# A decoder layer on one core: the FFN's first weights, factors and products as routines of the attention's event loop

## The chip, the core and the metric

The kernel runs on one core of a Trainium2 chip. The metric is the time of one execution on the device in microseconds (us). The core has five engines with instruction streams of their own: TensorE (PE in the profile; its weight loads are PEld), VectorE (DVE), ScalarE (ACT), GpSimd (POOL) and SyncE (SP, which here only issues transfers; ScalarE issues some too). Each engine works through its stream in order and waits on semaphores for the others.

## The reference, cut to what matters

One layer on 2048 tokens of width 1024, all in float32:

```python
h = rms_norm(x, norm1_g)
proj = h @ w_in
o_a = swa_sink_mixer(qa, ka, va, sinks, bias)        # 256 columns, window of 128
o_b = s5_mixer(proj[...], ...)                       # 512 columns, state space model + GLU
o_c = nsa_mixer(qc, kvc, gc, ...)                    # 256 columns: compressed, selected, window of 512
mixed = concat([rms_norm(o_a, g_a), rms_norm(o_b, g_b), rms_norm(o_c, g_c)])
x = x + mixed @ w_out
h2 = rms_norm(x, norm2_g)
hid = relu(h2 @ w_up)                                # 4096 columns
out = x + (hid * hid) @ w_down
```

## The kernel before, in words

Every float32 product is made of three matmuls: each operand is split into a high part (a cast to the matmul format on ScalarE) and a low part (a subtraction on VectorE), and high x high, high x low and low x high are added in PSUM. `split` (L1910) is this pair of instructions.

**Stages.** `phase_front` makes the projection and the state space model. A bias stage in `trunk` (L2365 on) makes the position biases, the windowed attention of group A and part of the GLU; its loads stand on SP's queue. `phase_mix` (L1156) makes the attention of group C (16 blocks of 128 queries), the last six blocks of the GLU and the output projection (16 "rows" of 128 tokens). `phase_up` (L1916) and `phase_down` (L2157) make the FFN.

**The event loop.** `phase_mix` writes its order out by hand. `Flow` (L1067) is a small planner that runs while the program is built. Every piece of work is a generator that yields `(engine, ns, function)` for a step, an `Event` to wait for, or a `Ring` (a number of buffers) to take a place of. `run` always takes the ready step with the earliest start by its costs, and among equals the one with the lowest rank. The calls of the functions in that order are the program's order on each engine (`tc.manual_schedule`); the costs serve for nothing else, and on the chip each engine waits for the real data. What is traced after that block (`phase_up`) is placed by the compiler's own scheduler, which may move it ahead between the instructions of the loop, in the order of its priority.

**The opening.** When the GLU is done, `opening` (L1230) runs `open_late` (L1200) as one step of VectorE with 5000 ns: it releases the GLU's memory, opens the pools of the output projection on the left side of SBUF, loads two vectors of gains (`g2t`, `wo_g`), makes two inverse roots of 16 numbers a partition on VectorE (`rsqrt_into`, L55, for group A's and B's norms), and sends the second through HBM to turn its layout (`r_d`, `r_t`, then `turn_rows` L1224 on TensorE). Then the 16 pieces of `w_out` are loaded and split (`weighed`, L1246).

**A row.** `finished(i)` (L1711) waits for the attention's output of block i in HBM (`oc`) and for the one buffer `mix`, loads 256 + 512 + 256 columns, scales the first two parts on POOL, squares the third on ScalarE into a tile `sq`, makes its inverse root on POOL (2300 ns in the plan), scales it, and turns the row in two halves on TensorE (bank `pt`), each split into `mh` and `ml`. `filled(i)` (L1759) makes 48 matmuls into two half rows, one bank `pw` each (L1781); for rows 14 and 15 the second half takes a bank `pq` of the attention. `added` (L1796) adds x on VectorE (L1803) and squares the sum on ScalarE with its output into the same PSUM bank (L1804); only then is the bank given back. `posted` (L1808) stores the row, makes the inverse root of the second norm, and for rows 0 to 7 turns and stores the normed row for the FFN.

Rows have a high rank number (100 i + 400 for i < 14), so that their matmuls fill gaps of the attention; some are left when the attention ends.

**The FFN.** Seven products of a Strassen-like scheme for each pair of 512 x 512 blocks, in the order 1, 6, 7, 5, 2, 4, 3. `fetch_factor` (L1996) loads a factor of the tokens (`fx`, 1 MB) from `hT` or `sums`, `refill` (L2000) splits it (`fh`, `fl`, 128x2048 each). `weights` (L2019) loads four blocks of `w_up` (`ur`), forms four sums on POOL (`fs`, L2037) and splits seven operands (`uh`, `ul`). `up` (L2052) makes the products: twelve matmuls each (L2066), into banks a, d, c, b (`pua` and so on). The first two factor fetches have a raised priority (`UP_HOIST`), and the compiler's scheduler also moves the first splits and weights ahead into the last rows.

## Time and profile before

| | us |
|---|---|
| median of 3 runs | 2488.86 (2485.08 to 2491.16) |
| the profiled execution | 2486.98 |
| its span, first to last instruction | 2484.9 |
| PE busy | 2397.5 |
| DVE busy | 1779.7 |
| ACT busy | 1321.3 |
| POOL busy | 1036.7 |

Times in the trace count from the first instruction. The opening lies at about 646, the end of the attention at about 1184, the FFN's first matmul at 1237 and the first of `phase_down` near 1880. In the lists of instructions a line gives the start, the length, the engine, the line of the code, the operation and out<-in; in square brackets stands how long the engine had been idle and what it then got. ACTq and SPq are transfers issued by ScalarE and SP. Matmuls are pipelined, so their lengths overlap: a 128x512 matmul at full clock starts about 0.23 us after the one before and is listed with 0.39.

### The profile page before, as it was taken

The numbers are of one execution on the slowest core, as the hardware profiler recorded it, in microseconds if no ns is written. First come the engines' busy times: TensorE is split into PE (matmuls) and PEld (weight loads), VectorE is DVE, ScalarE is ACT, GpSimd is POOL, SyncE is SP. The second block draws the span as 40 slices with busy tenths as digits, with TensorE's granted clock in tenths as the row PEclk, the third lists the DMA queues.
The fourth block names the chain that finished last, engine by engine and source line by source line (L and its number), as shares of the span: only waits on it lengthen the run. The fifth ranks groups of instructions, "written<-read, shape, count | busy, mean of one in ns | idle before, by whom it ended". The sixth has DMA issues, their size and how long they took to land.

```text
span 2484.9 us, 37987 instructions
## 1 busy us (share of the span) xinstructions
PE 2397.5 (96%) x12738; PEld 2059.6 (83%) x12738; DVE 1779.7 (72%) x3493; ACT 1321.3 (53%) x2756; POOL 1036.7 (42%) x1041
## 2 busy tenths in 40 slices
PE   8999998999899999999799999999999999999999
PEld 7899997777788888888688888788887888888887
DVE  7853875864777888888465566655557888889886
ACT  6443555765667767666355555444444444434442
POOL 0000223322243444231666674666654444445447
PEclk9999999999899999999999999999999999999999
DMA  7473334341322243212566667655548443444435
GB/s 233 137 257 118 105 99 108 105 149 48 112 76 71 85 127 111 67 39 68 166 204 193 191 191 225 207 152 151 153 130 287 133 124 97 132 139 127 127 102 196
DMA packets 402259, 344.45 MB, mean 139 GB/s; under 512 B 43622, under 2 KB 359020, under 8 KB 400112
## 3 DMA queue, kind: packets, MB, share of 16 engines
q1 hardware_dynamic: 341696, 288.23, 38.4%
q10 hardware_dynamic: 60368, 53.80, 6.9%
q8 instruction: 100, 1.64, 0.3%
q14 instruction: 95, 0.78, 0.1%
HBM read 227.39 MB, written 119.76 MB: 140 GB/s over the span
## 4 chain that ended last, share of the span: by engine, by line
PE 68%; DVE 3%; issue 3%; POOL 2%; DMA 2%; ACT 1%; ACTq 0%; SPq 0%; DVEq 0%; POOLq 0%
PE pdc L2245 7%; PE pdb L2245 7%; PE pda L2245 7%; PE pub L2066 6%; PE puc L2066 6%; PE pw L1781 6%; PE pua L2066 6%; PE pdd L2245 3%; PE pud L2066 3%; PE pos L1481 2%; PE pps L1448 2%; PE pow L1481 1%; PE pqs L1424 1%; PE pqs L1423 1%; PE ppw L1448 1%
## 5 line engine op out<-in xcount | busy, mean ns | idle before, releaser
L1912 ACT CAST v<-vr 128x512 fp32r<-128x512 f32 x224 | 139.3, 623 | 304.0 <-DMA vr<-vd 156.7
L1913 DVE TENSOR_TENSOR v<-vr,v 128x512 fp32r<-128x512 f32 x224 | 240.4, 1082 | 78.3 <-ACT v L1912 78.1
L2245 PE MATMUL pdc<-dw,v 128*128 128x512 f32 x768 | 187.3, 393 | 4.2 <-ACT dw L1912 2.8
L2245 PE MATMUL pdb<-dw,v 128*128 128x512 f32 x768 | 184.5, 389 | 0.0
L2245 PE MATMUL pda<-dw,v 128*128 128x512 f32 x768 | 184.5, 389 | 0.0
L2245 PEld LDWEIGHTS pdc<-dw,v 128*128 128x128 f32 x768 | 145.5, 190 | 36.0 <-ACT dw L1912 3.2
L548 POOL TENSOR_TENSOR t<-Q,E 128x508 f32<-128x508 f32 x16 | 22.1, 1381 | 364.5 <-ACT Q L528 326.4
L2245 PEld LDWEIGHTS pdb<-dw,v 128*128 128x128 f32 x768 | 144.2, 188 | 30.0
L2245 PEld LDWEIGHTS pda<-dw,v 128*128 128x128 f32 x768 | 144.2, 188 | 29.9
L1912 ACT CAST uh<-fs 128x512 fp32r<-128x512 f32 x124 | 76.3, 621 | 156.9 <-PE pub L2066 58.7
L1913 DVE TENSOR_TENSOR ul<-fs,uh 128x512 fp32r<-128x512 f32 x124 | 128.8, 1040 | 33.4 <-ACT uh L1912 33.1
L2037 POOL TENSOR_TENSOR fs<-ur,ur 128x512 f32<-128x512 f32 x62 | 86.8, 1400 | 156.0 <-DMA ur<-in_w_up 138.5
L1913 DVE TENSOR_TENSOR ul<-ur,uh 128x512 fp32r<-128x512 f32 x93 | 97.6, 1051 | 43.7 <-ACT uh L1912 41.1
L1781 PE MATMUL pw<-wo_h,mh 128*128 128x512 f32 x256 | 105.5, 412 | 10.4 <-ACT pw L1804 10.2
L2082 POOL TENSOR_TENSOR ev<-e,e 128x512 f32<-128x512 f32 x64 | 95.4, 1490 | 47.9 <-ACT e L2079 20.4
L1464 ACT CAST ths<-pps 128x512 fp32r<-128x512 f32 (+1 forms) x144 | 79.2, 563 | 64.5 <-PE pps L1448 53.9
L1469 DVE TENSOR_TENSOR tls<-pps,ths 128x512 fp32r<-128x512 f32 (+1 forms) x144 | 92.8, 657 | 17.2 <-ACT ths L1464 16.0
L1781 PE MATMUL pw<-wo_h,ml 128*128 128x512 f32 x256 | 104.3, 408 | 0.0
L2066 PE MATMUL pub<-fh,uh 128*128 128x512 f32 x256 | 101.1, 395 | 3.0 <-DVE e L2075 3.0
L1781 PE MATMUL pw<-wo_l,mh 128*128 128x512 f32 x256 | 103.7, 405 | 0.0
L2066 PE MATMUL puc<-fh,uh 128*128 128x512 f32 x256 | 100.2, 391 | 1.9 <-DVE eu L2075 1.9
L2066 PE MATMUL pua<-fh,uh 128*128 128x512 f32 x256 | 99.8, 390 | 1.5 <-ACT pw L1804 1.5
(560 smaller groups left out, 7777.7 us busy)
## 6 DMA issues: line engine op xcount, KB each, us to landing
vr<-vd SPq DMA_DIRECT2D x224, 256.0 KB
vd<-ev SPq DMA_DIRECT2D x128, 256.0 KB
ur<-in_w_up SPq DMA_DIRECT2D x124, 256.0 KB
vd<-e ACTq DMA_DIRECT2D x64, 256.0 KB
dr<-in_w_down SPq DMA_DIRECT2D x32, 512.0 KB
x<-in_x SPq DMA_DIRECT2D x16, 512.0 KB
mx<-in_x ACTq DMA_DIRECT2D x32, 256.0 KB
x<-mx ACTq DMA_DIRECT2D x32, 256.0 KB
```

The costliest lines, as they stand in the source:

```text
L1423: nc.tensor.matmul(pq[:, o:o + w], S["qA"][:, h], ka, start=True, stop=False)
L1448: nc.tensor.transpose(pt[:, j, hh], sls[hh][:, (b0 + j) * P:(b0 + j + 1) * P], C["ident"])
L1464: yield "ACT", cast_ns(n), lambda: nc.scalar.copy(th[:, 0:nb], pt[:, 0:nb])
L1469: t = yield "DVE", sub_ns(n), lambda: nc.vector.tensor_tensor(tl[:, 0:nb], pt[:, 0:nb], th[:, 0:nb], op=ALU.subtract)
L1481: nc.tensor.matmul(po_of(), v_of(b0 + j), tt[:, j].rearrange("p h q -> p (h q)"), start=b0 + j == 0 and n == 0, stop=b0 + j == nblk - 1 an ...
L1781: t = yield "PE", mm_ns(512), lambda: nc.tensor.matmul(pw[n], a[half][:, j], b[k][:, sl], start=k == 0 and m == 0, stop=k == NK - 1 and m ...
L1912: nc.scalar.copy(dh, src)
L1913: nc.vector.tensor_tensor(dl, src, dh, op=ALU.subtract)
L2037: nc.gpsimd.tensor_tensor(t, x, y, op=op)
L2066: nc.tensor.matmul(bank[b], w[:, k], h[o][:, k], start=first and k == 0 and n == 0, stop=k == HALF - 1 and n == 2, skip_group_check=True)
L2082: nc.gpsimd.tensor_tensor(tile_("v" + o), x, y, op=op)
L2245: nc.tensor.matmul(bank[b, q], x[:, q, j], y[:, j], start=first and j == 0 and n == 0, stop=j == 1 and n == 2, skip_group_check=True)
```

## The change: what it does

- `open_late` becomes a step of ScalarE's queue with 60 ns and only opens pools, now on the right side of SBUF. The gains are loaded once, in the bias stage (`gs`). The two inverse roots run on POOL in a routine `norms`; the turned one first.
- `finished` loads the first 768 columns of a row as soon as `mix` is free; the third part has a routine of its own (`load_oc`) that waits for the attention's output.
- The squares of a row write their unused output to a tile `junk` in SBUF. The bank `pw` is given back after the addition. Rows 14 and 15 no longer use the attention's banks.
- `attention_over` waits for the last block's output, closes the attention's pools and the biases' (`over`), opens a second `pw` bank and a new `pt` bank, and runs `phase_up`, now a generator, up to its first `yield`. Its weights, the fetches of five factors, the splits of three factors (in quarters) and the products 1, 6 and 7 are then routines of the event loop with the rank 100000 and more; the weight sums wait until row 15's first half is turned. Product banks come from two pools of four.
- The rest of `phase_up` is traced after the loop as before. `UP_HOIST` is gone.

```diff
-def phase_mix(tc, C, x, gains, B, cmp, w_out, out_norm_g, g2, pd, ..., oc_d, glu, release):
+def phase_mix(tc, C, x, gains, B, cmp, w_out, out_norm_g, g2, pd, ..., oc_d, glu, release, over, up):
...
+        def late_pool(name, bufs, **kw):
+            return ctx.enter_context(tc.tile_pool(name=name, bufs=bufs, reuse_waits="tile", side="right", **kw))
...
         def open_late():
 
             release()
-            fp = late["fp"] = pool("m_f", 1)
-            wp = pool("m_w", 1)
-            late["ps"] = pool("m_psw", 1, space=PSUM)
-            ps_o.append(pool("m_pso2", 1, space=PSUM))
+            fp = late["fp"] = late_pool("m_f", 1)
+            wp = late_pool("m_w", 1)
+            late["sm"] = late_pool("m_sml", 3)
+            late["small"] = small_of(late["sm"])
+            ps_w.append(late_pool("m_psw", 1, space=PSUM))
+            ps_o.append(pool("m_pso2", 1, space=PSUM, side="right"))
...
-            g2t = late["g2"] = fp.tile([P, NK], F32, name="g2t")
-            nc.sync.dma_start(g2t, g2[0].rearrange("(k p) -> p k", p=P))
-            go = late["go"] = wp.tile([P, NK], F32, name="wo_g")
-            nc.sync.dma_start(go, out_norm_g[0].rearrange("(k p) -> p k", p=P))
-            ra, rc = (fp.tile([P, NT], F32, name=n) for n in ("r_a", "r_c"))
-            rsqrt_into(nc, sm, ra, ss_a, 1.0 / 256, NT, "ra")
-            rsqrt_into(nc, sm, rc, ss_b, 0.25 / 512, NT, "ra")
-            nc.vector.tensor_scalar(rc, rc, 0.5, None, op0=ALU.mult)
-            nc.sync.dma_start(r_d.rearrange("(c s) -> c s", s=T16), rc)
+            late["junk"] = fp.tile([P, 512], F32, name="junk")
+
+        def row_norms():
+            rsqrt_into(nc, late["sm"], late["rc"], ss_b, 0.25 / 512, NT, "ra", nc.gpsimd)
+            nc.gpsimd.tensor_scalar(late["rc"], late["rc"], 0.5, 1.0, op0=ALU.mult, op1=ALU.mult)
...
-            yield "DVE", 5000, open_late
-            put(R["po"], flow.engines["DVE"])
-            fire(opened, flow.engines["DVE"])
+            t = yield "ACT", 60, open_late
+            put(R["po"], t)
+            spawn(norms(), 55, t)
+            fire(opened, t)
...
+        def norms():
+            yield "POOL", 3300, row_norms
+            t = yield "SP", 60, row_norms_out
+            spawn(rows_turned(), 60, t + 2 * DMA_NS)
+            yield "POOL", 3100, lambda: rsqrt_into(nc, late["sm"], late["ra"], ss_a, 1.0 / 256, NT, "ra", nc.gpsimd)
+            fire(norms_there, flow.engines["POOL"])
...
             yield opened
             box = {}
-            yield ev["oc"]
             yield R["mix"]
...
-                nc.scalar.dma_start(mix[:, 768:D], oc_d[rows])
-            t = yield "ACT", 180, load
+            t = yield "ACT", 120, load
+            spawn(load_oc(i, rows, box), rank, t)
...
+            yield box["oc"]
             dst = mix[:, 768:D]
...
-            yield "ACT", 630, lambda: nc.scalar.activation(sq, dst, AF.Square, accum_out=ss)
+            yield "ACT", 630, lambda: nc.scalar.activation(late["junk"][:, 0:256], dst, AF.Square, accum_out=ss)
...
+        def load_oc(i, rows, box):
+            box["oc"] = Event()
+            yield E[i]["oc"]
+            t = yield "ACT", 60, lambda: nc.scalar.dma_start(box["mix"][:, 768:D], oc_d[rows])
+            fire(box["oc"], t + DMA_NS + 700)
...
-                    alt = i >= ENDING and n
-                    yield R["pq"] if alt else R["pw"]
-                    p, tag, bufs = (ps_s, "pq", 2) if alt else (late["ps"], "pw", 1)
-                    pw[n] = p.tile([P, 512], F32, tag=tag, bufs=bufs, name=f"pw{i}{n}")
+                    yield R["pw"]
+                    bank = ps_w.pop(0)
+                    pw[n] = bank.tile([P, 512], F32, tag="pw", name=f"pw{i}{n}")
...
-            yield "DVE", 683, lambda: nc.vector.tensor_tensor(xt, xt, pw, op=ALU.add)
-            t = yield "ACT", 789, lambda: nc.scalar.activation(pw, xt, AF.Square, accum_out=ss[:, n:n + 1])
-            put(R["pq" if alt else "pw"], t)
+            t = yield "DVE", 683, lambda: nc.vector.tensor_tensor(xt, xt, pw, op=ALU.add)
+            ps_w.append(bank)
+            put(R["pw"], t)
+            t = yield "ACT", 820, lambda: nc.scalar.activation(late["junk"], xt, AF.Square, accum_out=ss[:, n:n + 1])
             fire(done, t)
...
+        def attention_over():
+
+            yield E[NT - 1]["oc"]
+            yield R["pt"]
+            box = {}
+
+            def switch():
+                c_att.close()
+                over()
+                ps_t[0] = late_pool("m_pst2", 1, space=PSUM)
+                ps_w.append(late_pool("m_psw2", 1, space=PSUM))
+                box.update(next(up))
+            t = yield "SP", 30, switch
+            put(R["pt"], t)
+            put(R["pw"], t)
+            first = {o: Event() for o in ORDER[:3]}
+            kept = {o: Event() for o in ORDER[:3]}
+            spawn(ffn_weights(box, kept), R_FFN, t)
+            prev = None
+            for o in ORDER[:5]:
+                spawn(ffn_factor(box, o, prev, first.get(o)), R_FFN + ORDER.index(o), t)
+                prev = first.get(o)
+            for o in ORDER[:3]:
+                spawn(ffn_product(box, o, first[o], kept[o]), R_FFN + ORDER.index(o), t)
+
+        def ffn_factor(box, o, prev, done):
+            yield R["fx"]
+            t = yield "SP", 60, lambda: box["fetch"](o)
+            if done is None:
+                return
+            yield landing(t, 1e6)
+            if prev is not None:
+                yield prev
+            box["slot"](o)
+            for k in range(HALF):
+                yield "ACT", 621, lambda: box["high"](o, k)
+                t = yield "DVE", 1060, lambda: box["low"](o, k)
+            put(R["fx"], t)
+            fire(done, t)
+
+        def ffn_weights(box, kept):
+            t = yield "SP", 240, box["load"]
+            yield landing(t, 1e6)
+            for o, n in box["weights"]:
+                if n is not None:
+                    yield E[NT - 1]["mh", 0]
+                    yield "POOL", 1440, n
+                spawn(ffn_kept(box, o, kept.get(o)), R_FFN + ORDER.index(o), flow.engines["POOL"] if n else flow.engines["SP"])
+
+        def ffn_kept(box, o, done):
+            yield "ACT", 621, lambda: box["keep_high"](o)
+            t = yield "DVE", 1060, lambda: box["keep_low"](o)
+            if done is not None:
+                fire(done, t)
+
+        def ffn_product(box, o, first, kept):
+            yield first
+            yield kept
+            for k in range(HALF):
+                yield "PE", 3 * mm_ns(512), lambda: box["product"](o, k)
...
-        ps_u = pool("f_psu", 2, space=PSUM)
+        ps_u = [pool("f_psu", 1, space=PSUM)]
...
+        yield {"fetch": lambda o: fetch_factor(0, o), "slot": lambda o: slot(0, o), "high": lambda o, k: high(0, o, k), "low": low_piece,
+               "load": load, "weights": order, "keep_high": keep_high, "keep_low": keep_low, "product": early}
+        ev = pool("f_e", 10)
+        es = pool("f_s", 3)
+        g2t = pool("f_g", 1).tile([P, PAD], F32, name="f_g2")
+        factors(ORDER[3:])
+        ps_u.append(pool("f_psu2", 1, space=PSUM))
+        for k, o in list(enumerate(ORDER))[3:]:
             refill(0, o)
...
+            gs = bp.tile([P, 2, NK], F32, name="g_late")
+            for j, src in enumerate((norm2_g, out_norm_g)):
+                nc.sync.dma_start(gs[:, j], src[0].rearrange("(k p) -> p k", p=P))
```

More of the change, by code (lines that the diff above doesn't have):

```diff
@@ L1153, with phase_mix @@
 DMA_NS = 2200
-def phase_mix(tc, C, x, gains, B, cmp, w_out, out_norm_g, g2, pd, oa_d, ob, x1, hT, xs, rr, rh, ss_a, ss_b, r_d, oc_d, glu, release):
+def phase_mix(tc, C, x, gains, B, cmp, w_out, out_norm_g, g2, pd, oa_d, ob, x1, hT, xs, rr, rh, ss_a, ss_b, r_d, oc_d, glu, release, over, up):
     nc = tc.nc
@@ L1743, in finished @@
                 yield R["pt"]
-                pt = ps_t.tile([P, 4, P], F32, tag="pt", name=f"ptx{i}{half}")
+                pt = ps_t[0].tile([P, 4, P], F32, tag="pt", name=f"ptx{i}{half}")
                 def turns():
@@ L1826, in posted @@
                 yield R["pt"]
-                pt = ps_t.tile([P, 4, P], F32, tag="pt", name=f"pth{i}{half}")
+                pt = ps_t[0].tile([P, 4, P], F32, tag="pt", name=f"pth{i}{half}")
                 def turns():
@@ new lines, in weights, with matmuls @@
+        def weights(p, f):
+            load, order, keep_high, keep_low, res = weight_steps(p, f)
+            load()
+            for o, n in order:
+                if n is not None:
+                    n()
+                keep_high(o)
+                keep_low(o)
+            return res
+        def matmuls(bank, u, o, k, first):
+            uh, ul = u[o]
+            for n, (w, h) in enumerate(((uh, hh), (uh, hl), (ul, hh))):
+                nc.tensor.matmul(bank, w[:, k], h[o][:, k], start=first and k == 0 and n == 0, stop=k == HALF - 1 and n == 2, skip_group_check=True)
@@ L2119, in phase_up, with early, low_piece @@
         steps = [(0, f) for f in reversed(range(NF))] + [(1, f) for f in range(NF)]
-        with tc.high_priority(offset=UP_HOIST):
-            for o in ORDER[:2]:
-                fetch_factor(0, o)
-        for k, o in enumerate(ORDER):
+        load, order, keep_high, keep_low, W["u"] = weight_steps(*steps[0])
+        banks = {}
+        def early(o, k):
+            b = dict(zip(ORDER, "adcbacb"))[o]
+            if k == 0:
+                banks[b] = ps_u[0].tile([P, NB], F32, tag=b, name=f"pu{b}e")
+            matmuls(banks[b], W["u"], o, k, True)
+        def low_piece(o, k):
+            low(0, o, k)
+            if k == HALF - 1:
+                rows.pop(o)
+        yield {"fetch": lambda o: fetch_factor(0, o), "slot": lambda o: slot(0, o), "high": lambda o, k: high(0, o, k), "low": low_piece,
[6 more added lines that the diff above has]
+        for k, o in list(enumerate(ORDER))[3:]:
             refill(0, o)
-            if k == 0:
-                W["u"] = weights(*steps[0])
             if k + 2 < 7:
@@ L2381, in trunk @@
             run(merge(swa, glu, [lambda: None] * 3 + c_steps + b_nsa))
-        phase_mix(tc, C, x, gains, B, cmp, w_out, out_norm_g, norm2_g, pd, oa_d, ob, x1, hT, sums, rr, rh_c, ss_a, ss_b, r_d, oc_d, rest, c_u.close)
-        c_b.close()
-        phase_up(tc, C, x1, rr, norm2_g, hT, sums, w_up, vd)
+        up = phase_up(tc, C, x1, rr, norm2_g, hT, sums, w_up, vd)
+        phase_mix(tc, C, x, gains, B, cmp, w_out, gs[:, 1], gs[:, 0], pd, oa_d, ob, x1, hT, sums, rr, rh_c, ss_a, ss_b, r_d, oc_d, rest, c_u.close, c_b.close, up)
+        for _ in up:
+            pass
         phase_down(tc, x1, w_down, vd, out)
```

155 lines of the change are left out of this document (79 added, 76 removed).

## The prediction

> **What bounds the kernel now.** I read the page's totals first, then the time in stretches of 50 us, and then the waits of TensorE in the two stretches that fall behind.
>
> ```profile
> span 2484.9 us, 37987 instructions
> PE 2397.5 (96%) x12738; PEld 2059.6 (83%) x12738; DVE 1779.7 (72%) x3493; ACT 1321.3 (53%) x2756; POOL 1036.7 (42%) x1041
> ...
> 650.00:700.00 50.00, 38.37 (x215) 33.38 (x216) 43.33 (x129) 35.78 (x93) 16.78 (x31) 0.83 0.41 130
> 1150.00:1200.00 50.00, 42.18 (x270) 36.78 (x269) 33.25 (x65) 30.02 (x55) 21.62 (x33) 0.95 0.49 152
> 1200.00:1250.00 50.00, 43.31 (x191) 34.72 (x190) 19.18 (x21) 16.21 (x26) 30.06 (x55) 0.98 0.47 163
> ...
> PE ptqc L845 <- DVE otc L1522: 5.9, 1, 5.9
> PE ptow L1517 <- DVE kAw L1370: 2.6, 1, 2.6
> ...
> PE pw L1781 <- ACT pw L1804: 9.1, 3, 6.5
> ```
>
> TensorE is busy 96% of the span, so it is the bound, and reordering can win only from the 87.4 us in which it stands still and from what a reduced clock costs. (The columns of a stretch: length, busy time of PE, PEld, DVE, ACT, POOL with instruction counts, granted clock, DMA share, GB/s.) Two stretches are poor: around 650, where the late pools are opened, and from 1184 to 1237, where the last rows are finished. The waits (total, times, longest) are for 644 to 707 and for 1184 to 1240.
>
> **The opening.** Three stretches, and the instructions on VectorE that TensorE waited for:
>
> ```profile
> 648.00:654.70 6.70, 0.82 (x6) 0.49 (x4) 5.81 (x30) 1.29 (x5) 0.52 (x1) 0.82 0.83 192
> 654.70:671.50 16.80, 12.71 (x60) 11.26 (x60) 14.33 (x43) 12.65 (x34) 5.42 (x9) 0.66 0.32 106
> 671.50:692.00 20.50, 17.66 (x112) 14.67 (x112) 18.82 (x42) 18.00 (x44) 10.87 (x21) 1.00 0.49 161
> ...
> 647.75 0.17 DVE L42 TENSOR_SCALAR rah<-ss_a 128x16 f32<-128x16 f32 x1
> ...
> 653.90 0.17 DVE L1218 TENSOR_SCALAR r_c<-r_c 128x16 f32<-128x16 f32 x1
> 653.99 0.69 DVE L1522 TENSOR_TENSOR otc<-ptoc,wc 128x512 f32<-128x512 f32 x1
> ...
> 666.09 0.17 DVE L1257 COPY r_b<-ptr 128x16 f32<-128x16 f32 x1
> ...
> 654.11 0.34 SPq L1219 DMA_DIRECT2D r_d<-r_c  x1
> ...
> 1221.20 0.19 POOL L43 TENSOR_SCALAR nr<-nqh 128x1 int32<-128x1 int32 x1
> 1221.50 0.34 POOL L46 TENSOR_SCALAR nqt<-nr,nqh 128x1 f32<-128x1 f32 x1
> ```
>
> The opening puts 29 small instructions (14 for each of two inverse roots, and one halving) on VectorE in one piece, from 647.75 to 654.07: 6.3 us. The eviction `otc` stands behind them, and TensorE waits 5.9 us for it. The change moves all 29 to POOL. **Removed: 5.9 us of waiting.** VectorE is busy 18.82 of the 20.50 us that follow, so no more than its own 6.3 us can be won there; I do not expect the 2.6 us wait to go, since the sixteen weight splits behind it stay. The lower end is 3 us, if half of the freed time is lost again to that queue. The upper end adds the clock: 12.71 us of busy time at 0.66 would take 8.4 at full clock, 4.3 less, so 5.9 + 4.3 = 10.2. I take 6.0, near the plain wait, because in that stretch VectorE (14.33 of 16.80) sets the pace with TensorE.
>
> The clock has a rule. The Trainium skill, TensorE: Matmul & The Clock Gate, Part 1, says that the clock falls to half after about 3.4 us without work and returns after about as long of dense work. This trace agrees as to the fall (0.82, then 0.66 behind the 5.9 us gap); by the rule the second figure would go too, and the opening would give the 10.2.
>
> On POOL the nearest rows are steps of 0.30 us (1221.20 to 1221.50) and, with the same gap of 0.11, of 0.45 (0.34 busy), so 15 for `rc` take 4.5 to 6.8 us and all 29 take 8.7 to 13.1. POOL is busy 0.52 + 5.42 of the 23.5 us, which hides them; without that cover 13 us would stand ahead of `oc` sums. From the store of `r_d` to `r_b` went 12.0 us; 647.75 + 6.8 + 12.0 = 666.6 against 666.09 now: rows are ready no later than before, to half a microsecond. **Cost: 0.**
>
> **Moved loads.** The two gain loads leave the opening and go on SP's queue to the bias stage:
>
> ```profile
> 647.20 0.65 SPq L1214 DMA_DIRECT2D wo_g<-in_out_norm_g  x1
> ...
> 393.57 0.43 SPq L2369 DMA_DIRECT2D c_wmask<-in_k_wmask  x1
> 397.50 0.37 SPq L826 DMA_DIRECT2D hnhn<-pb  x1
> ```
>
> Two issues are at most 1.3 us ahead of the mask, where SP issues nothing for 3.5 us afterwards. Cost 0; without that gap 1.3.
>
> **The end of the attention.** Four stretches, then the chain:
>
> ```profile
> 1184.70:1198.90 14.20, 6.47 (x29) 4.84 (x28) 8.60 (x10) 6.24 (x15) 13.59 (x16) 0.86 0.64 201
> 1198.90:1210.00 11.10, 8.45 (x33) 6.51 (x34) 7.68 (x7) 5.42 (x7) 10.13 (x13) 0.87 0.43 136
> 1210.00:1225.00 15.00, 12.42 (x58) 9.94 (x58) 2.07 (x3) 2.41 (x8) 10.94 (x27) 1.00 0.72 261
> 1225.00:1237.30 12.30, 10.80 (x48) 8.60 (x46) 2.07 (x3) 1.97 (x6) 1.92 (x7) 1.00 0.11 31
> ...
> 1195.56 1.95 DVE L1913 TENSOR_TENSOR ul<-fs,uh 128x512 fp32r<-128x512 f32 x2 [1.80 <-ACT uh L1912]
> 1197.43 0.68 DVE L1803 TENSOR_TENSOR mx<-mx,pw 128x512 f32<-128x512 f32 x1
> ...
> 1198.97 0.79 PE L1781 MATMUL pw<-wo_h,mh 128*128 128x512 f32 x1 [6.50 <-ACT pw L1804]
> 1203.65 0.60 PE L1749 MATMUL ptx<-c_ident,mix 128*128 128x128 f32 x4
> 1237.33 0.50 PE L2066 MATMUL pua<-fh,uh 128*128 128x512 f32 x1 [1.53 <-ACT pw L1804]
> ...
> 1200.74 4.49 DVE L1913 TENSOR_TENSOR fl<-fx,fh 128x2048 fp32r<-128x2048 f32 x2 [0.63 <-ACT fh L1912]
> ...
> 1203.19 2.25 POOL L46 TENSOR_SCALAR nqt<-nr,nqh 128x1 f32<-128x1 f32 x1
> ...
> 1189.24 0.84 ACTq L1723 DMA_DIRECT2D mix<-oa_d  x1
> 1195.95 0.41 ACT L1735 ACTIVATE sq<-mix 128x256 f32<-128x256 f32 x1
> 1220.32 0.42 ACT L1735 ACTIVATE sq<-mix 128x256 f32<-128x256 f32 x1 [10.58 <-DMA mix<-oc_d]
> 1237.19 3.70 ACT L1912 CAST fh<-fx 128x2048 fp32r<-128x2048 f32 x2
> ...
> 1239.11 4.52 DVE L1913 TENSOR_TENSOR fl<-fx,fh 128x2048 fp32r<-128x2048 f32 x2 [2.59 <-ACT fh L1912]
> ...
> L1912 ACT CAST uh<-fs 128x512 fp32r<-128x512 f32 x124 | 76.3, 621 | 156.9 <-PE pub L2066 58.7
> L1913 DVE TENSOR_TENSOR ul<-fs,uh 128x512 fp32r<-128x512 f32 x124 | 128.8, 1040 | 33.4 <-ACT uh L1912 33.1
> ```
>
> From 1184.7 on TensorE has only rows 13, 14 and 15 of the output projection to do, and then the FFN. Up to 1237.3 it does 6.47 + 8.45 + 12.42 + 10.80 = 38.1 us of work in 52.6: **14.5 us idle**. The reduced clock costs 0.14 x 6.47 + 0.13 x 8.45 = 2.0 more. So 16.5 us are there to be won, and a row takes (38.1 - 2.0)/3 = 12.0 us of TensorE.
>
> Part by part. (1) The bank of a half row is given back after the addition, and the square goes to a junk tile in SBUF: from 1197.43 + 0.68 = 1198.11 to the matmul at 1198.97 are 0.9 us, three times in the 9.1. (2) From the switch on there are two such banks, so the rest of those waits goes. The 6.5 us one arose because VectorE, in order, ran the FFN's weight splits (1195.56) before the addition (1197.43); as routines with the last rank these now stand behind the rows. (3) The FFN's first bank no longer lies where the last row's was: 1.53 us. (4) The first 768 columns of a row are loaded and scaled without waiting for the attention's output, and only the square waits for the last 256, where ScalarE now stands 10.58 us.
>
> What stays is the row's own chain, since `mix` has one buffer: load to square 6.7 us (1189.24 to 1195.95), in all 14.4 us to the first turn (1203.65), against 12.0 us of matmuls of the row before. I put it half way, so 1.2 us is open in each of two rows, and 0.7 for the last addition (0.68): 3.1. **Gain 16.5 - 3.1 = 13.4.** The upper end is 16.5.
>
> The lower end: both rows keep 2.4 us (4.8), and the three FFN products fill those holes early. They are the cover for the next factor's split, whose cast starts at 1237.19 and whose difference ends about 1239.11 + 2.26 = 1241.4; against the last matmul (1237.33 - 1.53 = 1235.8) that is 5.6 us in which TensorE would have nothing. 16.5 - 4.8 - 5.6 = 6.1. This stall is what is late next; I leave it out, since by rank the products come after the rows wherever these are ready.
>
> The half way has a row against it: a POOL step of 0.34 us took 2.25 at 1203.19, while VectorE ran two factor splits from 1200.74 to 1205.23. The Trainium skill, GPSIMD Engine Reference, Key points, has POOL share its SBUF interface with VectorE and contend with its two-input instructions, which the splits are. The trace agrees; by that rule the splits, now routines of the same loop, would hold the rows' roots again and 14.4 us a row would stay, as in rival (a).
>
> Added: splits in quarters. Three factors cost ScalarE 3 x (4 x 0.62 - 1.85) = 1.9 us and VectorE at most 3 x (4 x 1.04 - 2.26) = 5.7 us more; both are busy about 2 of 15 us at 1210 and again at 1225, which hides them. The switch on SP places the four weight loads and the factor loads behind the last `oc` store in SP's order only; what holds them is the release of attention tiles, as before.
>
> **The middle.** In 707 to 1140 the order is planned anew, with rows ready earlier:
>
> ```profile
> 707.00:1140.00 433.00, 424.41 (x2841) 377.52 (x2840) 355.82 (x1058) 293.77 (x710) 165.31 (x352) 1.00 0.26 80
> ```
>
> Only 8.6 us are idle. I take 0, between +4 (half of it) and -8 (as much again lost).
>
> **The sum.** 6.0 + 13.4 = 19.4 us off. The profiled execution took 2486.98 us (span 2484.9): 2467.6. It lies 1.9 under the runs' median of 2488.86, so the forecast is 2469 for the median. Its own range: gains of 9.1 (3.0 + 6.1) to 26.7 (10.2 + 16.5), so 2462 to 2480.
>
> **The rivals.** (a) The row chain still sets the end: 14.4 us a row and an early fill, 6.1 instead of 13.4. For it: one `mix` buffer, and the POOL step of 2.25 us. Against: by rank the splits come after the rows. Time 2488.9 - 12.1 = 2477. (b) The clock comes back in the opening as well and the middle gives 4: 19.4 + 4.3 + 4 = 27.7, 2461. For it: 0.66 in 16.8 us. Against: VectorE is as full as TensorE there. (c) Nothing: the new order in the middle loses what the ends win, about 19 us over eleven blocks, 1.8 each; 2488. For it: every order from 647 on changes. Against: only 8.6 idle in 433 us by the same planner. (d) Slower, by one mechanism: the separate load of the last 256 columns stands on ScalarE's queue right behind the store it reads, and the square behind it; ScalarE is in order, so casts and exponentials queue there, as in the 10.58 us row, when the load lands later than planned. With 2 us lost in each of 15 rows: 30 - 19.4 = 11 us slower, 2499; it decides from 1.3 us a row. Against: in the trace this wait occurs once in sixteen rows.
>
> **Chances.** Forecast 0.54, (a) 0.19, (b) 0.08, (c) 0.09, (d) 0.10. A measurement of this kernel tells 0.3%, 7.5 us, from no change: faster means under 2481.4. Forecast and (b) are faster, (a) nearly always (0.17 of 0.19): 0.79; same 0.11; slower 0.10. The range runs from 2459 to 2488, which holds (a), (b) and half of (c).
>
> **What would show it.** Right: no group of `r_a`, `r_c` on VectorE near 648 and the `ptqc` wait gone; clock near 1.0 there; no wait of `pw` above 1 us after the attention; the last row's matmul some 19 us earlier than 1235.8; 36 products on `pua`, `pud`, `puc` just around it and `pub` without a wait over 1 us. Wrong: a wait of `pub` on `fl` of 4 us or more (the cover), waits of TensorE on `ths` or `sls` behind a `mix` load (d), or more than 12 us idle between 700 and 1140 (c).

## The result and the profile after

The changed kernel takes 2467.8 us (median of 4 runs, 2463.2 to 2471.8) against 2487.0 for the kernel before on the same chip (4 runs): a ratio of 0.9921, 95% interval 0.9905 to 0.9936, so 19.2 us less. In a second set, below, the ratio was 0.9914 (0.9901 to 0.9928), 21.3 us less. The forecast was 2469 with 19.4 us less. The sum came out; two of its terms did not, and by luck their errors cancelled.

The page's totals of the changed kernel:

```profile
span 2466.8 us, 37987 instructions
PE 2399.6 (97%) x12738; PEld 2061.1 (84%) x12738; DVE 1776.0 (72%) x3473; ACT 1322.2 (54%) x2765; POOL 1038.4 (42%) x1070
```

Its time in stretches (length; busy time of PE, PEld, DVE, ACT, POOL; granted clock, DMA share, GB/s), cut at its own landmarks, the last product of the attention (1177.5) and the last row's matmul (1209.8):

```profile
646.00:707.00 61.00, 54.13 (x308) 46.66 (x307) 49.71 (x131) 44.30 (x115) 28.76 (x66) 0.86 0.40 126
707.00:1140.00 433.00, 431.80 (x2889) 385.36 (x2889) 360.05 (x1068) 300.01 (x722) 171.96 (x372) 1.00 0.27 82
...
1177.50:1209.80 32.30, 30.95 (x144) 25.30 (x145) 15.39 (x22) 14.47 (x31) 20.61 (x38) 1.00 0.57 192
1209.80:1240.00 30.20, 26.37 (x93) 18.78 (x92) 24.05 (x22) 16.92 (x24) 19.25 (x17) 0.83 0.72 234
```

The same stages of the kernel before (the middle stands in the prediction). They are cut at 1184.7, as in the prediction; the last product of its attention starts at 1181.6, and TensorE is busy in between:

```profile
646.00:707.00 61.00, 48.19 (x277) 41.67 (x276) 51.53 (x155) 43.19 (x112) 21.59 (x37) 0.86 0.39 118
...
1184.70:1235.60 50.90, 37.94 (x165) 29.89 (x164) 19.73 (x21) 15.30 (x30) 36.57 (x60) 0.93 0.50 170
1235.60:1262.00 26.40, 24.35 (x105) 19.37 (x105) 19.64 (x18) 17.50 (x23) 13.07 (x12) 1.00 0.59 190
```

What a stage loses is its length less busy time times clock. Opening: 61 - 48.19 x 0.86 = 19.6 before, 14.4 after (12.0 in a second profile, at a clock of 0.94). Middle: 8.6 before, **1.2 after**. Last rows: 50.9 - 37.94 x 0.93 = 15.6 before, 1.4 after. The 26 to 30 us behind the last row: 2.1 before, 30.2 - 26.37 x 0.83 = **8.3 after**, of which 3.8 are idle and 4.5 the clock. So 5.2 + 7.4 + 14.2 are won and 6.2 given back.

A second reckoning doesn't need the clock: three landmarks in TensorE's instructions by tile (name, count, shortest/median/longest ns, first and last start). Before, then after:

```profile
L642 PE MATMUL gpm<-glu_bh,glu_ones x32: 388/397/501, 433.0 to 645.1; 128*128 128x512 f32 x32
...
L1781 PE MATMUL pw<-wo_h,ml x256: 387/394/628, 676.0 to 1235.4; 128*128 128x512 f32 x128
...
L2245 PE MATMUL pdc<-dw,v x768: 389/389/793, 1871.4 to 2476.7; 128*128 128x512 f32 x192
```

```profile
L642 PE MATMUL gpm<-glu_bh,glu_ones x32: 387/397/496, 435.1 to 647.7; 128*128 128x512 f32 x32
...
L1802 PE MATMUL pw<-wo_h,ml x256: 387/395/578, 675.5 to 1209.4; 128*128 128x512 f32 x128
...
L2360 PE MATMUL pdc<-dw,v x768: 389/389/796, 1854.0 to 2459.0; 128*128 128x512 f32 x192
```

From the end of the GLU to the last row (**A**) it is 1235.4 - 645.1 = 590.3 before and 561.7 after; from there to the first matmul of `phase_down` (**B**) 636.0 and 644.6. A is 28.6 shorter, B is 8.6 longer. The end of the GLU itself lies between 642.9 and 647.7 in all the profiles of this study, on both sides of the 645.1 before; what precedes it was not edited except for two small loads, so it is left out. The same three rows were read for every run, from its one profiled execution (that of run 1 was the fastest of its five, 2467.5):

| kernel | median us | ratio to before | A | B | A + B |
|---|---|---|---|---|---|
| before | 2486 to 2487 | 1 | 590.3 | 636.0 | 1226.3 |
| after, first and second profile | 2467.8, 2464.7 | 0.9921, 0.9914 | 561.7, 561.5 | 644.6, 643.4 | 1206.3, 1204.9 |
| 1 norms on VectorE | 2472.8 | 0.9945 | 571.3 | 637.8 | 1209.1 |
| 2 bank back late | 2481.8 | 0.9981 | 581.2 | 640.5 | 1221.7 |
| 3 before + early bank | 2477.0 | 0.9966 | 580.8 | 636.6 | 1217.4 |
| 4 row loaded whole | 2470.5 | 0.9939 | 566.5 | 642.5 | 1209.0 |
| 5 FFN behind the loop | 2474.1 | 0.9951 | 573.4 | 640.6 | 1214.0 |
| 6 one bank at the end | 2468.9 | 0.9930 | 565.8 | 644.4 | 1210.2 |
| 7 sums late | 2464.9 | 0.9913 | 561.0 | 642.9 | 1203.9 |
| 8 and loads on ScalarE | 2464.8 | 0.9916 | 559.3 | 645.3 | 1204.6 |
| 9 three factor buffers | 2492.3 | 1.0026 | 560.3 | 672.3 | 1232.6 |
| 10 three, and sums late | 2493.0 | 1.0027 | 561.9 | 671.9 | 1233.8 |
| 11 four loads on SP | 2463.1 | 0.9910 | 561.7 | 645.0 | 1206.7 |

The intervals of the ratios are 0.0008 to 0.0016 to either side. After the table, "the changed kernel" means A + B of 1205.6, the mean of its two profiles.

The waits of TensorE in the opening of the changed kernel (total, times, longest):

```profile
PE pow L1497 <- ACT thw L1480: 2.8, 1, 2.8
PE pos L1497 <- ACT ths L1480: 1.3, 1, 1.3
```

The 5.9 us wait for `otc` and the 9.1 us of `pw` for the squares are gone. At the end the FFN's products wait in their place, 1.9 us for `fl` and 1.6 for `fh` (shown with runs 7 to 10).

### The profile page after: what moved, and what is told of

Same layout as the page of the kernel before. It is cut to its first block, busy times and chain, and to the rows that moved or that the text cites. A ratio compares the mean times of both kernels' runs of the same rounds, so it can differ in the third digit from the quotient of the medians.

```text
span 2466.8 us, 37987 instructions
## 1 busy us (share of the span) xinstructions
PE 2399.6 (97%) x12738; PEld 2061.1 (84%) x12738; DVE 1776.0 (72%) x3473; ACT 1322.2 (54%) x2765; POOL 1038.4 (42%) x1070
## 4 chain that ended last, share of the span: by engine, by line
PE 71%; DVE 2%; issue 2%; DMA 2%; POOL 1%; ACT 1%; SPq 0%; ACTq 0%; DVEq 0%; POOLq 0%
PE pdc L2360 7%; PE pdb L2360 7%; PE pda L2360 7%; PE pw L1802 7%; PE pub L2151 6%; PE puc L2151 6%; PE pua L2151 6%; PE pdd L2360 3%; PE pud L2151 3%; PE pos L1497 3%; PE pps L1464 2%; PE pqs L1439 1%; PE pqs L1440 1%; PE pow L1497 1%; PE ppw L1464 1%
## 5 line engine op out<-in xcount | busy, mean ns | idle before, releaser
L548 POOL TENSOR_TENSOR t<-Q,E 128x508 f32<-128x508 f32 x16 | 21.3, 1334 | 365.6 <-ACT Q L528 334.7
L2121 POOL TENSOR_TENSOR fs<-ur,ur 128x512 f32<-128x512 f32 x62 | 92.9, 1499 | 161.1 <-DMA ur<-in_w_up 135.2
L2151 PE MATMUL pub<-fl,uh 128*128 128x512 f32 x256 | 101.1, 395 | 0.3 <-DVE fl L2090 0.3
L2151 PE MATMUL pub<-fh,ul 128*128 128x512 f32 x256 | 101.0, 394 | 0.0
```

Of the source, the lines that this page charges most:

```text
L2121: nc.gpsimd.tensor_tensor(S[n], x, y, op=op)
L2151: nc.tensor.matmul(bank, w[:, k], h[o][:, k], start=first and k == 0 and n == 0, stop=k == HALF - 1 and n == 2, skip_group_check=True)
```

## The experiments

**1. The opening.** The 29 instructions go back to VectorE.

```diff
-            rsqrt_into(nc, late["sm"], late["rc"], ss_b, 0.25 / 512, NT, "ra", nc.gpsimd)
+            rsqrt_into(nc, late["sm"], late["ra"], ss_a, 1.0 / 256, NT, "ra")
+            rsqrt_into(nc, late["sm"], late["rc"], ss_b, 0.25 / 512, NT, "ra")
...
-            yield "POOL", 3300, row_norms
+            t = yield "DVE", 5000, row_norms
+            fire(norms_there, t)
```

> The changed kernel with one part undone: the 29 small instructions of the two inverse roots run again on VectorE, in one piece, as one 5000 ns step of the opening (everything else stays changed). The prediction's theory: TensorE waits about 5.9 us near 648 for the eviction otc behind them, and the time is 5 to 6 us above the changed kernel's 2467.8, so about 2473. Rival, the gap is made up later: the rows that fill gaps in the middle absorb it, TensorE's idle time from 646 to 707 grows by 5 to 6 us but the end moves by less than 2 us, 2468 to 2470.

Measured 2472.8, ratio 0.9945 (0.9931 to 0.9959). TensorE's longest wait from 640 to 707:

```profile
PE ptqc L845 <- DVE otc L1538: 5.9, 1, 5.9
```

The wait is back to the tenth, and the median is where the theory put it. The landmarks add something: the last row is 9.7 us later (A), and 6.2 of these come back in B. A delay of the rows is here partly paid for by the step behind them.

**2. The bank.** The square writes to the bank again, which is given back after it.

```diff
-            t = yield "DVE", 683, lambda: nc.vector.tensor_tensor(xt, xt, pw, op=ALU.add)
-            ps_w.append(bank)
-            put(R["pw"], t)
-            t = yield "ACT", 820, lambda: nc.scalar.activation(late["junk"], xt, AF.Square, ...)
+            yield "DVE", 683, lambda: nc.vector.tensor_tensor(xt, xt, pw, op=ALU.add)
+            t = yield "ACT", 789, lambda: nc.scalar.activation(pw, xt, AF.Square, ...)
+            ps_w.append(bank)
+            put(R["pw"], t)
```

> The changed kernel with one part undone: the square of a half row writes into its PSUM bank again and the bank is given back only after it (rows 0 to 15). The prediction's theory: the early return is worth 0.9 us three times at the end of the attention and nothing in the middle: about 2470.5, idle time of TensorE from 707 to 1140 stays at 1 to 2 us. Rival, the bank is what closed the small gaps of the middle (8.6 us idle before, 1.2 in the changed kernel): idle there returns to 6 to 9 us, and with the 2.7 at the end the time is 2475 to 2478.

Measured 2481.8, ratio 0.9981 (0.9972 to 0.9989): above both forecasts. The middle and the stretch to the last row, and TensorE's longest wait behind 1190:

```profile
707.00:1140.00 433.00, 425.36 (x2833) 377.24 (x2833) 354.59 (x1054) 293.36 (x710) 170.90 (x364) 1.00 0.26 81
...
1177.50:1226.40 48.90, 43.35 (x199) 35.09 (x198) 21.17 (x31) 19.54 (x43) 28.27 (x57) 0.93 0.54 183
```

```profile
PE pw L1802 <- ACT pw L1825: 4.4, 1, 4.4
```

The middle is idle 7.6 us again, against 1.2, and the stretch up to the last row loses 48.9 - 43.35 x 0.93 = 8.6, against 1.4. **So the middle's gain is the bank's**, and so is half of the end's: 16 us of A + B hang on these four lines.

**3. The bank alone.** The same lines, and the tile in SBUF, put into the kernel before, with nothing else.

```diff
...
-            yield "DVE", 683, lambda: nc.vector.tensor_tensor(xt, xt, pw, op=ALU.add)
-            t = yield "ACT", 789, lambda: nc.scalar.activation(pw, xt, AF.Square, ...)
+            t = yield "DVE", 683, lambda: nc.vector.tensor_tensor(xt, xt, pw, op=ALU.add)
             put(R["pq" if alt else "pw"], t)
+            t = yield "ACT", 820, lambda: nc.scalar.activation(late["junk"], xt, AF.Square, ...)
```

> The kernel before with one part of the change alone: the bank of a half row is given back after the addition, and both squares of a row write their unused output to a tile in SBUF. Theory after the second experiment (the bank fills the middle): the 8.6 us idle from 707 to 1140 fall to 1 to 3 us, and the 0.9 us three times at the end go too: 8 to 10 us off, 2476 to 2478. Rival, the whole of the 14 us that its undoing cost belongs to it: about 2472. Rival, the middle needs the earlier rows and norms as well: idle there stays above 6 us, 2482 to 2485.

Measured 2477.0, ratio 0.9966 (0.9953 to 0.9978): the first theory, and nearly half of the whole change's gain. The middle, and the 30 us behind the last row:

```profile
707.00:1140.00 433.00, 430.85 (x2878) 383.58 (x2879) 358.84 (x1062) 297.03 (x719) 171.12 (x369) 1.00 0.26 83
...
1225.20:1255.20 30.00, 29.63 (x129) 23.71 (x128) 24.32 (x23) 20.64 (x27) 16.97 (x15) 1.00 0.58 185
```

The middle falls to 2.1 us idle. The step to the FFN loses only 0.4 here: the FFN is traced behind the loop as in the kernel before, and the rows end 19 us later (A) than in the changed kernel.

What TensorE waited for in the middle, two lines of the kernel before, then one of run 3:

```profile
PE pos L1481 <- DVE tls L1469: 1.4, 2, 0.7
PE pw L1781 <- ACT pw L1804: 1.1, 2, 0.5
...
PE pos L1481 <- DVE tls L1469: 0.4, 1, 0.4
```

All of TensorE's waits in the middle come to 8.2 us before and to 1.9 in run 3. Only 1.1 of the 8.2 name the bank; most of the others name operands of the attention, whose code is the same in both.

Up to the last row the bank alone wins little. From 1184.7 on run 3 loses 40.5 - 31.84 x 0.83 = 14.1, against 15.6 before:

```profile
1184.70:1225.20 40.50, 31.84 (x132) 25.30 (x132) 17.74 (x18) 13.46 (x24) 27.50 (x40) 0.83 0.54 185
...
PE ptx L1750 <- DVE ml L1753: 6.8, 2, 6.6
```

VectorE stood at two of the FFN's splits (from 1204.0, 4.95 us) before it formed the row's `ml`. So half of the end's gain needs the bank (run 2), but the bank wins it only together with the routines.

**4. The row's load.** `finished` waits for `oc` again and issues its three transfers together.

```diff
+            yield ev["oc"]
             yield R["mix"]
...
-            t = yield "ACT", 120, load
-            spawn(load_oc(i, rows, box), rank, t)
+                nc.scalar.dma_start(mix[:, 768:D], oc_d[rows])
+            t = yield "ACT", 180, load
...
-            yield box["oc"]
```

> The changed kernel with one part undone: a row's load waits for the attention's output again, and its three transfers are issued together. The prediction's theory: the early load shortens only the rows' chain at the end; without it 14.4 us a row stand against 12.0 of matmuls in two rows, 2 to 5 us lost, 2470 to 2473, and the middle stays at 1 to 2 us idle. Rival one: rows that are ready earlier are what fills the middle; its idle time returns to 6 to 9 us and the time is 2473 to 2477. Rival two, case (d) of the prediction: the separate load holds ScalarE's queue, and without it the time falls by 2 us or more, under 2466.

Measured 2470.5, ratio 0.9939 (0.9927 to 0.9952); A + B is 3.4 us longer. The interval of the ratio overlaps that of the changed kernel, so the loss rests on the landmarks. The middle stays at 433 - 431.27 = 1.7 idle, and A is 4.9 longer. The time is the theory's, rival one falls, and rival two has the wrong sign.

The theory's mechanism isn't shown, though. Row 15's first and third transfer in the changed kernel, then the first in run 4:

```profile
1186.02 0.36 ACTq L1738 DMA_DIRECT2D mix<-oa_d  x1
1186.96 0.41 ACTq L1778 DMA_DIRECT2D mix<-oc_d  x1
...
1185.99 0.48 ACTq L1739 DMA_DIRECT2D mix<-oa_d  x1
```

The load goes out at 1186.0 in both, behind row 14's second turn (1184.5 and 1184.9), which is the last to read `mix`. In the changed kernel it is 4.6 us behind the store of the attention's last output (1181.4), so at this row nothing was loaded ahead of it; nor at row 14, whose three transfers go out together from 1166.3 to 1167.2. Where the 4.9 us arise is open.

**5. The FFN's routines.** After the switch nothing is spawned; loads, splits and products are traced behind the loop.

```diff
-            spawn(ffn_weights(box, kept), R_FFN, t)
...
-                spawn(ffn_product(box, o, first[o], kept[o]), R_FFN + ORDER.index(o), t)
...
+        with tc.high_priority(offset=1500):
+            for o in ORDER[:2]:
+                fetch_factor(0, o)
+        for k, o in enumerate(ORDER):
             refill(0, o)
+            if k == 0:
+                W["u"] = weights(*steps[0])
```

> The changed kernel with one part undone: after the switch of the pools, with its second bank for half rows, the FFN's first loads, splits and products are no routines of the loop but are traced behind it as before, with the raised priority of the first two fetches, so that the compiler's scheduler places them between the rows' instructions. The prediction's theory: the weight splits stand ahead of the last rows' additions on VectorE again and TensorE loses up to 6.5 us there, 2470 to 2474. Rival, the cover: with the first splits made early the step from the last row to the FFN loses nothing, as before (2.1 us idle from 1235.6 to 1262 in the kernel before, against 3.8 us idle and 4.5 us of clock from 1209.8 to 1240 in the changed one), and two banks hide the additions: 2461 to 2465, faster than the changed kernel.

Measured 2474.1, ratio 0.9951 (0.9938 to 0.9965): the upper end of the theory's range. The rows are late (A 11.8 longer than the changed kernel's), and B gives back only 3.4. TensorE's waits from 1170 to 1260, and POOL's instructions:

```profile
PE puc L2142 <- ACT fh L2077: 4.4, 1, 4.4
PE ptx L1765 <- POOL mix L1753: 2.9, 1, 2.9
PE ptx L1765 <- POOL mix L1747: 2.1, 1, 2.1
```

```profile
1193.17 2.72 POOL L1747 TENSOR_SCALAR mix<-mix,r_b 128x512 f32<-128x512 f32 x1
1195.86 3.42 POOL L2112 TENSOR_TENSOR fs<-ur,ur 128x512 f32<-128x512 f32 x1
```

The right number for another reason: TensorE waits not for the additions that the theory named, which two banks cover, but for POOL's scaling of `mix`. The FFN's sums stand on POOL's queue between the last row's steps (two of them, 4.7 us, ahead of its root at 1200.6). The routines put them behind these steps. The rival is right that two banks cover the additions and wrong in the rest: the products wait 4.4 us for a split even so.

**6. One bank at the end.** The second bank of the switch isn't opened.

```diff
-                ps_w.append(late_pool("m_psw2", 1, space=PSUM))
...
-            put(R["pw"], t)
```

> The changed kernel without the second bank for half rows that is opened at the switch; the early return of the one bank and the FFN routines stay. The prediction's theory: with the routines behind the rows the additions are no longer held, so one bank costs 0.9 us less its overlap for each of the last four half rows, 2 to 3.5 us, 2469 to 2471. Rival, the additions still stand behind the splits on VectorE in places (the last but one took its bank at 1196.2 to 1196.9, the last at 1204.3): a half row waits 2 us or more, 2472 to 2475. Rival, what is lost ahead of the last row comes back since the factors are late anyway: under 2468.5.

Measured 2468.9, ratio 0.9930 (0.9917 to 0.9942), beside 2464.7 for the changed kernel in the same set: 4.2 us, a little over the theory's 2 to 3.5. All of it is in A (4.2 longer), as for a bank it should be, but from 1140 to the last row the waits that name `pw` rise only from 0.5 to 1.8 us; the rest is not accounted for.

> The changed kernel itself, unchanged, beside the other three of this set: 2466 to 2469. In its profile the clock from 646 to 707 tells whether the dip of the opening (0.86 in the first profile) belongs to the program or to the execution: theory, to the execution, since five variants with the same opening showed 0.86 to 0.97 there.

That run of the changed kernel took 2464.7 (2464.6 to 2467.0), with a clock of 0.94 from 646 to 707 where its first profile had 0.86.

**7 to 10. The step to the FFN.** This is what took back 8 us. Single instructions of the changed kernel, in order of time within each group:

```profile
1218.25 0.51 PE L2151 MATMUL puce<-fl,uh 128*128 128x512 f32 x1 [1.93 <-DVE fl L2090]
1222.53 0.80 PE L2151 MATMUL pub<-fh,uh 128*128 128x512 f32 x1 [1.60 <-ACT fh L2086]
...
1213.53 1.77 DVE L2090 TENSOR_TENSOR fl<-fx,fh 128x512 fp32r<-128x512 f32 x1
1217.51 0.68 DVE L2090 TENSOR_TENSOR fl<-fx,fh 128x512 fp32r<-128x512 f32 x1
...
1214.72 1.73 POOL L2121 TENSOR_TENSOR fs<-ur,fs 128x512 f32<-128x512 f32 x1
...
1197.48 0.34 SPq L2078 DMA_DIRECT2D fx<-sums  x1
1207.24 7.90 SPq L2117 DMA_DIRECT2D ur<-in_w_up  x3
1215.24 0.46 SPq L2078 DMA_DIRECT2D fx<-sums  x1
...
1220.58 1.90 ACT L2086 CAST fh<-fx 128x2048 fp32r<-128x2048 f32 x1 [0.67 <-DMA fx<-sums]
```

The three products are done by about 1221, but factor 7's splits ran at 1.77 us each while POOL formed the second weights' sums (0.68 once POOL was done), and factor 5's load stood on SP's queue behind three loads of those weights. Run 7 makes the sums wait for factor 7's split (the first edit); run 8 also issues the loads of factors 5 and 2 on ScalarE's queue (the second):

```diff
+                if (p, f) == steps[1] and n == 1:
+                    nc.gpsimd.tensor_scalar(S[n][:, 0, 0:1], hl[ORDER[2]][:, HALF - 1, 3, P - 1:P].bitcast(F32), ...)
...
+            late_one = ORDER.index(o) >= 3
+            t = yield "ACT" if late_one else "SP", 60, lambda: box["fetch"](o, nc.scalar if late_one else None)
```

> The changed kernel, with the POOL sums of the second set of weights made to wait for the last quarter of factor 7's split (one added instruction of one column on POOL reads it). In the changed kernel these sums ran from 1210.1 to 1216.5, and the splits of VectorE beside them took 1.77 us each instead of 0.68. Theory, contention of the two makes factor 7 late: its splits take 0.7 us each again, TensorE's 1.9 us wait for fl goes, and the load of factor 5, which stands on SP's queue behind loads that wait for these splits, is issued earlier: 2463 to 2466. Rival, the splits are late by their order on VectorE alone: 1.9 us stay, 2467 to 2469. Rival, the sums are then late themselves: a new wait of 2 us or more between 1225 and 1245, 2468 to 2471.

> The same, and in addition the loads of factors 5 and 2 are issued on ScalarE's queue, where no load of the second weights stands ahead of them (in the changed kernel factor 5's load was issued at 1215.2, eleven us after the buffer was free). Theory, the step to the FFN loses 3.8 us idle and 4.5 us of clock because factors 7 and 5 are late: both gone, idle of the 30 us behind the last row under 1.5 us at a clock of 1.00, 2459 to 2463. Rival, the issue holds ScalarE's queue and casts behind it are late: 2467 or more. Rival, the transfer itself is slow beside the loads of the weights and nothing changes against the run before: 2463 to 2466.

Measured 2464.9 (0.9899 to 0.9926) and 2464.8 (0.9902 to 0.9929): neither can be told from the changed kernel. Yet each did its part where it was made. With the sums late factor 7's splits take 0.69 to 0.72 us and the 1.9 us wait for the last of them is gone, but TensorE waits for the next pieces instead (two of its waits in run 7 from 1170 to 1260, then the split of factor 5):

```profile
PE puce L2153 <- ACT fh L2086: 2.4, 1, 2.4
PE pub L2153 <- DVE fl L2090: 2.2, 1, 2.2
...
1217.06 3.37 DVE L2090 TENSOR_TENSOR fl<-fx,fh 128x2048 fp32r<-128x2048 f32 x1 [1.76 <-ACT fh L2086]
```

The contention was moved and not removed: POOL's late sums (from 1217.0 on) now ran beside factor 5's split, which took 3.37 us against 2.30 in the changed kernel.

With the loads on ScalarE's queue too, factor 5 is in time, and TensorE waits 6.2 us in one piece for factor 2, whose load went out at 1209.4 and whose cast began at 1217.4:

```profile
1217.36 1.90 ACT L2087 CAST fh<-fx 128x2048 fp32r<-128x2048 f32 x1 [5.08 <-DMA fx<-hT]
...
PE puae L2154 <- ACT fh L2087: 6.2, 1, 6.2
```

So contention and queue order are real, but what they cost is taken by whichever factor comes next: the reading is that the supply of 1 MB factors through two buffers sets this step. For it speak the loads of the third and fourth factor in the kernel before, whose rows ended 26 us later: they went out at 1187.8 and 1212.3, against 1197.5 and 1215.2 in the changed kernel.

```profile
1187.79 0.34 SPq L1998 DMA_DIRECT2D fx<-sums  x1
1212.34 0.46 SPq L1998 DMA_DIRECT2D fx<-sums  x1
```

Runs 9 and 10 give the factors a third buffer; in run 10 the sums are late as well. The buffer had to be paid for in SBUF, by one buffer in each of three pools and half of a small tile of gains (64 columns, not shown):

```diff
-        xp = pool("f_x", 2)
+        xp = pool("f_x", 3)
-        st = pool("f_st", 5)
+        st = pool("f_st", 4)
-        ru = pool("f_ru", 6)
+        ru = pool("f_ru", 5)
...
-        ev = pool("f_e", 10)
+        ev = pool("f_e", 9)
```

> The changed kernel with three buffers for factors (fx) instead of two; to make room, the pools of w_up blocks, of their sums and of results have one buffer fewer each (ru 5, st 4, ev 9). Theory, the step to the FFN is bound by the supply of factors (a load takes 8 to 9 us from issue to cast and two buffers hold it back): factor 7's load starts near 1174 instead of 1197.5 and factor 5's near 1197.5 instead of 1215.2; the wait of pub for fh (1.6 us) and the clock behind it (4.4 us) go, the wait for factor 7's last split (1.9 us) stays; 2462 to 2465. Rival, the smaller pools cost the FFN 3 us or more from 1240 on: 2467 to 2472. Rival, the order of the casts on ScalarE holds factor 5 all the same: 2466 to 2469.

> The same with three buffers, and the sums of the second weights wait for factor 7's split as in the run with the late sums. Theory: both causes of the loss behind the last row are gone, idle of the 30 us behind it under 2 us at a clock of 1.00 against 3.8 and 0.83, 2459 to 2463, faster than the changed kernel. Rival, the next factor (2) or the second weights are late in turn, 3 us or more idle in that stretch: 2464 to 2467.

Measured 2492.3 and 2493.0, both slower than the kernel before. In run 9 the 30 us behind the last row lose 30 - 26.72 x 0.89 = 6.2, against 8.3 without the third buffer; in run 10 they lose 30 - 22.45 x 0.89 = 10.0. B grows by 28 us in both, and in run 9 the products wait 15.7 us from 1235 on for evictions of their banks (L2186); which of the smaller pools is behind that was not tried:

```profile
1205.20:1235.20 30.00, 26.72 (x101) 19.93 (x100) 27.77 (x24) 20.10 (x28) 20.42 (x16) 0.89 0.68 221
...
1206.60:1236.60 30.00, 22.45 (x83) 16.33 (x82) 21.42 (x20) 16.66 (x24) 17.45 (x17) 0.89 0.62 204
```

```profile
PE pua L2151 <- ACT e L2186: 15.7, 3, 5.7
```

So the reading is argued and not shown (run 9 speaks for it and run 10 against, and the smaller pools may bear on both), and whether a third buffer from other memory would win the 6 to 8 us of this step is open. No version beat the changed kernel by more than the intervals.

**11. The new stall of the opening.** In the changed kernel TensorE waits 2.8 us for a cast `thw`, and of the 4.3 us ahead of it ScalarE spends most on issuing eight transfers, of which the second to the fourth and the cast are shown:

```profile
650.14 1.54 ACTq L1251 DMA_DIRECT2D oraw<-in_w_out  x3
...
654.08 0.37 ACT L1480 CAST thw<-ppw 128x256 fp32r<-128x256 f32 x1 [0.68 <-DMA oraw<-in_w_out]
```

```diff
-                    t = yield "ACT", 60, lambda: nc.scalar.dma_start(raw, w_out[...])
+                    q, eng = ("SP", nc.sync) if k < 2 else ("ACT", nc.scalar)
+                    t = yield q, 60, lambda: eng.dma_start(raw, w_out[...])
```

> The changed kernel with the first four loads of w_out in the opening issued on SP's queue instead of ScalarE's. In the changed kernel ScalarE issues eight transfers from 649.8 to 654.1, about 0.45 us each, and TensorE waits 2.8 us for a cast behind them. Theory, these issues took the place of VectorE's 29 instructions as the cause of the stall: four fewer take 1.9 us of it, 2465 to 2466, and if the clock stays up as well 2461 to 2464. Rival, the cast waits for a transfer and not for the issues: no change, 2467 to 2469.

Measured 2463.1, ratio 0.9910 (0.9897 to 0.9924), which is not told apart from the changed kernel; A is 561.7 as before the edit. The wait for `thw` fell from 2.8 to 1.3; one for `ths` is 1.8, where the two profiles of the changed kernel have 1.3 and 2.3. The theory's mechanism is there, its 2 us are not.

## Why the prediction was right, and where it was not

**The opening, 6.0 (3.0 to 10.2): right.** The wait is gone, and putting the instructions back costs 5.0 and 8.1 us against the two medians of the changed kernel, 3.5 in A + B. POOL took 4.3 us for the first root (4.5 to 6.8 predicted) and 10.6 for both with a sum of `oc` between them (8.7 to 13.1), from 651.2 to 655.6 and to 661.9. The two gain loads show no cost beyond the 2 to 3 us by which the end of the GLU varies. What was wrong is the sign it named, a clock near 1.0: it was 0.86. And the 2.6 us wait that was to stay went, with 2.8 us behind ScalarE's transfer issues in its place, a queue that the working of the opening hadn't looked at.

**The middle, 0 (+4 to -8): the step that failed.** It put the term at 0 without giving a reason, and bounded the gain by half of the 8.6 us. 7 us were won. Runs 2 and 3 show that it is the bank's. The reading, which no run takes further apart: with the one bank held, the rows' matmuls, which are the filler, cannot start while the last sum is added and squared, and just then the attention's own waits show. (The target of the square moves together with the bank's return in both runs, so the two are not told apart.) Part (1) saw the early return only where `pw` is named in a wait (0.9 us, three times); it works on 32 half rows.

**The last rows, 16.5 less 3.1: better than said.** 1.4 us are idle instead of 3.1. The parts are mis-sized among themselves: the bank was put at 2.7 and half of the 14.2 hangs on it (run 2), though alone it wins at most 1.5 there (run 3). The FFN block of the loop is worth 8 us (run 5), the second bank 4 (run 6), the row's separate load 3 to 5 (run 4); they overlap, so they don't add.

Part (4) misread its row. The last row's load went out at 1209.1, once row 14's last turn (1208.1) had read `mix`; the attention's last output had been stored at 1188.4. So the 10.58 us of ScalarE were no wait for the attention's output, and a load that does not wait for it could not win them. What the rows gained is an earlier start: before, row 14's load went out 7.6 us behind the attention's last product (1189.2, 1181.6), in the changed kernel 10.9 ahead of it (1166.3, 1177.2). With the bank alone it goes out 25.7 us ahead (run 3), with all but the bank 1.7 (run 2).

**The cover, left out: the second step that failed.** "By rank the products come after the rows" was right, but the rows ended 26 us earlier and the factors did not come earlier at all. The prediction priced this stall at 5.6 us of waiting, as the lower end, called it what is late next, and left it out; it costs 8 (B); of the 8.3 us lost behind the last row, 4.5 are clock, which the working did not count. Of its signs, a wait of 4 us for `fl` did not come, but neither did a `pub` without a wait over 1 us: `puce` waits 1.9 us for `fl` and `pub` 1.6 for `fh`.

**The sum.** A was to fall by about 6.0 + 13.4 with B unchanged; A fell by 28.6 and B rose by 8.6. The time is right since the middle (7) made up for the step to the FFN (8). Nothing in the working ties the two together: this is luck, a right total from a partly wrong account. **The quarter splits** were put at no cost behind 2 of 15 us busy; beside POOL's sums they took 1.77 us instead of 0.68. What that costs isn't shown: run 7 moved the contention to the next factor, and the time stayed.

**The rivals.** (a) falls, but not because the chain is short: row 15 took 9.9 us from its load (1186.0) to its first turn (1196.0), against 11.8 before (1209.1 to 1220.8), and row 14 took 15.4 (1166.3 to 1181.8), mostly while the attention was still running. (b) was half right, in the middle. (c) has the wrong sign, and (d) is refuted by run 4; a cast behind transfers on ScalarE's queue does cost 2.8 us, but in the opening. The contention that (a) leaned on does exist: with the routines it hits the FFN's splits (1.77 us) and one step of the last row's root (1.30 us instead of 0.34, at 1193.4), without them the row's scaling (`mix` by `r_b`, 2.72 us in run 5). Both agree with the Trainium skill, GPSIMD Engine Reference, Key points.

## What to carry to other kernels

Where one engine's work is the filler for another's gaps, the resource that the filler gives back late (here a PSUM bank held through an addition and a square) costs on every use, and shows in waits that name other things; count its uses, not its waits. A stage that ends earlier wants its successor's inputs earlier too: look up when their transfers were issued, and price the step as if they came no sooner. What one part is worth depends on the others: alone, the bank won at most 1.5 us ahead of the last row, and its absence from the whole change cost 7 there. And split the result by landmarks before believing a sum that fits.

## What the runs showed of the hardware

The clock after a gap differs from execution to execution of the same program. Both profiles of the changed kernel stand still for 2.8 to 2.9 us near 652. In the first the granted clock of the following 16.5 us was 0.63, in the second 0.80; run 8, with a gap of 2.5 us there, kept 0.90 over 17.7 us.

```profile
654.50:671.00 16.50, 13.68 (x64) 12.64 (x65) 15.22 (x43) 14.62 (x40) 12.71 (x32) 0.63 0.45 146
...
653.70:671.00 17.30, 13.43 (x71) 11.81 (x72) 16.25 (x46) 15.25 (x42) 13.20 (x32) 0.80 0.45 149
...
649.30:667.00 17.70, 13.73 (x78) 10.92 (x79) 17.12 (x49) 16.62 (x45) 12.92 (x33) 0.90 0.47 163
```

The Trainium skill, TensorE: Matmul & The Clock Gate, Part 1, has activity judged in windows of about 3.4 us that run free of the program, so that the moment of a change varies; that fits the spread. Its table asks for a whole idle window ahead of a fall, and these gaps are shorter: here the runs go further than the page. With one buffer fewer in each of three pools of the FFN, and a third one for the factors, B was 28 us longer (runs 9 and 10), more than this whole change won.
